# Two SwiGLU down projections in different forms, and the stores and sums of the gate stages on other engines

## The chip, the core and the metric

The kernel runs on one core of one Trainium2 chip. The metric is the device time of one execution in microseconds (us), median of several. The core has five engines that each work through a queue of their own in order: PE (TensorE, matmuls, with its weight loads PEld), DVE (VectorE), ACT (ScalarE), POOL (GpSimd) and SP (SyncE, which here issues nearly all DMAs). They meet through semaphores.

## The reference

A decoder trunk of two layers in float32, with 1024 tokens of 1024 features and an FF width of 2816. The first layer mixes tokens by sliding-window attention, the second by stick-breaking attention, and each is followed by a SwiGLU. Scales, shifts and gates of every sub-layer come from the conditioning `c` by `ada_w` (adaLN).

```python
def swiglu(h, w_gate, w_up, w_down):
    return (jax.nn.silu(h @ w_gate) * (h @ w_up)) @ w_down

def reference(x, c, ...):
    cond = jax.nn.silu(c)
    for i in range(DEPTH):                       # DEPTH = 2
        mod = (cond @ ada_w[i] + ada_b[i])[:, None, :]
        sh1, sc1, g1, sh2, sc2, g2 = jnp.split(mod, 6, axis=-1)
        h = rmsnorm(x, norm1_g[i]) * (1.0 + sc1) + sh1
        y = ...                                  # attention of layer i
        x = x + g1 * y
        h = rmsnorm(x, norm2_g[i]) * (1.0 + sc2) + sh2
        x = x + g2 * swiglu(h, w_gate[i], w_up[i], w_down[i])
    return x
```

## The kernel before, in words

Every matrix product is made of float32 operands split in two: ACT casts the high part (`sh` L629, `dah` and `dbh` L308), DVE subtracts it to get the low part (`sl` L630, `dal` and `dbl` L309), and three matmuls, high by high, high by low and low by high, stand for one (`mm3`, each matmul recorded at L108). The order of the matmuls is written out by hand and chained; the other engines' order comes from a scheduler that keeps to the order of the code where priorities don't differ. A pool of n buffers makes the n+1st user wait until the first is done.

A **gate stage** (`gates`, one for each layer) computes silu(h w_gate) * (h w_up) in 11 chunks of 256 FF columns. The product of a chunk is cut in 2 x 2 blocks, and seven block products stand in place of eight: seven for the gate and seven for the up weights, 12 matmuls each, 168 a chunk. On PE a chunk is three stretches by its PSUM banks: `psd` (X, 48 matmuls), `psz` (Y: T2, T3 and N4, 72) and `pst` (Z: T1 and B22, 48). POOL makes the sums of weight blocks that these products need, in the ring `rg` of seven buffers (`block_sums` L804 to L806, `t2_product` L812); DVE adds up the results (`u2` L814, `u3` L851, `p1` L854, L858, L861), and ACT and DVE make silu and product (L864, L865; `g11` L843, L844). The four results of a chunk, A11, A12, A22 and `g11`, lead to the seven left operands of the down projection: A11, A12 and A22 themselves, and the four sums S1 (POOL, L867), S2 (L871), S4 (L873) and S3 (L875). All seven are stored to DRAM by `store` (L829) on SP's queue.

At the start of each chunk `down_sums` (L902) loads two 128-row blocks of w_down (L907) into the pool `ad` of two 512 KB buffers, POOL makes four sums of their quarters (L910), and two stores on SP's queue bring them to DRAM (`wT`, L915 and L916). In layer 0 each chunk also issues five steps of the adaLN products that later stages need (`ada_step`, 56 in all): a load of 512 KB into the same pool `ad` (L262), an accumulation on DVE (L268, or L265 for the first of a group of eight), and after a group of eight some small matmuls against `ones`.

A **down projection** (`down` L918, the same code for both layers) is again seven block products, 924 matmuls: each loads a left operand from `hidS` and a right one from w_down or `wT` (L923, pool `raw` with five buffers), splits them, and multiplies over 22 FF blocks. The results are multiplied by the gate's row when they leave PSUM (L959) and added to the residual `xacc` (L964), the last of them just before `finish` stores a row block. After layer 0 `norm_b` (L1066) normalises each row block of the residual (L1074 on DVE) and transposes it on PE (L116) for the second layer's projections, whose weights are loaded and split ahead (L309, L312).

## Time and profile before

| | |
|---|---|
| median of the runs shown | 2538.48 us (3 runs: 2553.88, 2538.48, 2538.34) |
| the profiled execution's own time | 2545.3 us |
| its span in the profile | 2543.6 us |
| granted TensorE clock, mean | 0.96 of full speed |
| busy in the span: PE, DVE, ACT, POOL | 91%, 65%, 43%, 35% |
| gates of layer 0 | 479.67 to 960.88 us |
| first down projection, PE | 973.56 to 1186.20 us |
| gates of layer 1 | 1895.46 to 2319.60 us |
| second down projection, PE | 2326.66 us to the end |

The profile is of one execution. Its view by stretches gives busy time of each engine in each stretch, the number of instructions in brackets, the granted TensorE clock as a share of full speed, the DMA engines' share and the rate. The view of waits gives for each engine and line what it waited for: total, times and the longest. The timeline gives start, duration, engine, line, operation, output and inputs, with the idle time before it and what ended that in square brackets. A row of several instructions has an x and their count. PE's neighbouring matmuls overlap, so what one costs is read from a long row of them and not from its own duration. Names such as `f`, `p`, `rg` are those of tiles; `f` and `p` are results of a gate stage's products.

### The profile page before, as it was taken

How to read it: one execution, taken by the hardware profiler on the slowest of the kernel's cores; microseconds unless marked ns; L12 is line 12 of the kernel's file. 1: busy time of each engine (PE TensorE's matmuls, PEld its weight loads, DVE VectorE, ACT ScalarE, POOL GpSimd, SP SyncE). 2: the span in 40 equal slices, each digit the busy share in tenths (PEclk: the TensorE clock that was granted, in tenths of full speed). 3: DMA queues.
4: the chain of work that ended last, by engine and by line, in shares of the span. 5: the costliest groups of instructions: out<-in, count | busy, mean ns of one | idle time of the engine just before them, and what ended most of it. 6: DMA issues, size and time to landing. Idle time of an engine off the chain costs nothing. (4 is left out here: it accounts for less than half of the span.)

```text
span 2543.6 us, 31733 instructions
## 1 busy us (share of the span) xinstructions
PE 2326.9 (91%) x11140; PEld 1903.1 (75%) x11140; DVE 1642.7 (65%) x2315; ACT 1106.1 (43%) x2109; POOL 898.9 (35%) x847
## 2 busy tenths in 40 slices
PE   6798799799889897999999999998979989998999
PEld 6677677577777776887788888877758767887887
DVE  6678866855566665755676766687565645554864
ACT  4487733422222223433566666673343322333431
POOL 2443524234645530001244444441514574541000
PEclk9799899899999998999999999999979999999999
DMA  8113488345566547762222222236813564226753
GB/s 283 50 51 120 126 219 260 108 137 167 198 190 207 194 145 274 243 198 91 60 59 59 59 55 56 58 96 156 240 59 103 169 224 141 95 96 218 255 190 140
DMA packets 229855, 371.85 MB, mean 146 GB/s; under 512 B 15536, under 2 KB 135488, under 8 KB 229696
## 3 DMA queue, kind: packets, MB, share of 16 engines
q1 hardware_dynamic: 229072, 369.69, 46.2%
q8 instruction: 88, 1.44, 0.2%
q14 instruction: 71, 0.58, 0.1%
q10 hardware_dynamic: 624, 0.14, 0.0%
HBM read 264.39 MB, written 96.99 MB: 142 GB/s over the span
## 5 line engine op out<-in xcount | busy, mean ns | idle before, releaser
L629 ACT CAST sh<-rg 128x512 fp32r<-128x512 f32 x308 | 190.5, 622 | 644.8 <-PE psz L108 251.2
L630 DVE TENSOR_TENSOR sl<-rg,sh 128x512 fp32r<-128x512 f32 x308 | 289.5, 942 | 130.1 <-ACT sh L629 125.2
L108 PE MATMUL psd<-hth,whl 128*128 128x512 f32 x768 | 302.1, 412 | 0.1
L1182 POOL TENSOR_TENSOR bb<-bb,nb 128x895 f32<-128x895 f32 (+7 forms) x128 | 172.7, 1352 | 240.9 <-DVE nb L1180 152.2
L1180 DVE TENSOR_TENSOR_SCAN nb<-nb,ones 128x896 f32<-128x896 f32 (+7 forms) x128 | 194.1, 1519 | 45.2 <-ACT nb L1173 44.8
L108 PE MATMUL psz<-hT,sh 128*128 128x512 f32 x352 | 146.9, 420 | 50.5 <-DVE f L814 24.8
L804 POOL TENSOR_TENSOR rg<-rg,rg 128x512 f32<-128x512 f32 x44 | 60.7, 1380 | 340.5 <-DMA rg<-in_w_up_dram 262.3
L108 PEld LDWEIGHTS psd<-hth,whl 128*128 128x128 f32 x768 | 145.3, 189 | 21.5 <-issue 0.7
L308 ACT CAST dah<-raw 128x1024 fp32r<-128x1024 f32 x84 | 82.5, 982 | 165.5 <-PE psa L108 77.2
L108 PE MATMUL psd<-htl,whl 128*128 128x512 f32 x384 | 151.0, 395 | 0.0
L119 DVE TENSOR_TENSOR al<-pst,ah 128x512 fp32r<-128x512 f32 x160 | 108.4, 684 | 62.1 <-ACT ah L1203 59.0
L108 PE MATMUL psz<-lT,sh 128*128 128x512 f32 x352 | 146.1, 415 | 1.9 <-DVE lT L119 1.8
L108 PE MATMUL psz<-hT,sl 128*128 128x512 f32 x352 | 144.6, 411 | 1.2 <-DVE sl L630 1.2
L309 DVE TENSOR_TENSOR dal<-raw,dah 128x1024 fp32r<-128x1024 f32 x84 | 95.2, 1133 | 70.4 <-ACT dah L308 69.4
L108 PE MATMUL psd<-hB,sh 128*128 128x512 f32 x352 | 137.8, 391 | 2.3 <-ACT p L799 2.3
L108 PE MATMUL psd<-hB,sl 128*128 128x512 f32 x352 | 137.2, 390 | 1.2 <-DVE sl L630 1.2
L268 DVE SCALAR_TENSOR_TENSOR acc<-ada,condT,acc 128x1024 f32<-128x1024 f32 x77 | 106.5, 1384 | 49.1 <-DMA ada<-in_ada_w_dram 48.5
L108 PE MATMUL psd<-lB,sh 128*128 128x512 f32 x352 | 137.4, 390 | 0.0
L108 PEld LDWEIGHTS psz<-hT,sh 128*128 128x128 f32 x352 | 70.3, 201 | 74.9 <-issue 27.1
L309 DVE TENSOR_TENSOR dbl<-raw,dbh 128x1024 fp32r<-128x1024 f32 x84 | 95.0, 1131 | 44.4 <-ACT dbh L308 43.7
L1173 ACT ACTIVATE nb<-psz 128x448 f32<-128x448 f32 (+3 forms) x192 | 95.7, 498 | 60.4 <-PE psz L108 57.3
L1203 ACT CAST ah<-pst 128x512 fp32r<-128x512 f32 x160 | 94.0, 593 | 47.5 <-PE pst L116 45.5
(340 smaller groups left out, 6606.8 us busy)
## 6 DMA issues: line engine op xcount, KB each, us to landing
ada<-in_ada_w_dram SPq DMA_DIRECT2D x96, 512.0 KB, 4.5
dw<-in_w_down_dram SPq DMA_DIRECT2D x44, 512.0 KB, 4.2
rg<-in_w_gate_dram SPq DMA_DIRECT2D x44, 512.0 KB, 4.8
rg<-in_w_up_dram SPq DMA_DIRECT2D x44, 512.0 KB, 4.8
wT<-dw SPq DMA_DIRECT2D x44, 512.0 KB, 3.2
raw<-wT SPq DMA_DIRECT2D x40, 512.0 KB, 5.3
raw<-hidS SPq DMA_DIRECT2D x40, 512.0 KB, 4.4
hidS<-f SPq DMA_DIRECT2D x64, 256.0 KB, 2.1
```

The lines of the kernel that those rows point to most:

```text
L108: chained(nc.tensor.matmul(o, l, r, start=start, stop=stop, skip_group_check=more))
L119: return nc.vector.tensor_tensor(o, a, h.bitcast(F32), op=ALU.subtract)
L268: i = nc.vector.scalar_tensor_tensor(a, wt, condT[:, j : j + 1], a, op0=ALU.mult, op1=ALU.add)
L308: nc.scalar.copy(h, raw)
L309: (eng or nc.vector).tensor_tensor(l, raw, h.bitcast(F32), op=ALU.subtract)
L629: nc.scalar.copy(hv, src)
L630: nc.vector.tensor_tensor(lv, src, hv.bitcast(F32), op=ALU.subtract)
L804: nc.gpsimd.tensor_tensor(A[1, 0], A[1, 0], A[1, 1], op=ALU.add)
L1173: nc.scalar.activation(nb[:, s0 : s0 + e], pz[:, 0:e], AF.Sigmoid, scale=-1.0)
L1180: nc.vector.tensor_tensor_scan(rv, rv, ones[:, 0:1].to_broadcast([P, L]), initial=1.0, op0=ALU.mult, op1=ALU.mult)
L1182: nc.gpsimd.tensor_tensor(bb[:, 0 : L - 1], bb[:, 0 : L - 1], nb[:, 1:L], op=ALU.mult)
L1203: nc.scalar.copy(ah_, pt)
```

## The change

In layer 1 the stores of a gate stage (L829 in the kernel before, and `wT` L915 and L916) go from SP's to POOL's DMA queue, and the four sums S1 to S4 from POOL to DVE. In layer 0 `down_sums` and the four sums are no longer done, and the four results go to a DRAM list `hid` by SP's queue (L847 and L870 in the kernel after). The first down projection is `down_rounds`: six rounds over the 22 FF blocks (4, 4, 4, 4, 4 and 2), in each of which two loads of 512 KB a block (the block of `hid`, 128 rows of w_down), a multiplication of the w_down rows by the gate's row on DVE and two splits precede 16 groups of matmuls, 1056 in all; each group is added from PSUM to the residual on DVE, and `finish` follows a row block's last add. The second projection keeps the block products.

```diff
--- before.py
+++ after.py
@@ -826,9 +826,10 @@
 
         def chunk(c):
             def store(n, t):
-                nc.sync.dma_start(hidS[n, c // 2][:, c % 2], t)
-
-            down_sums(l, c)
+                nc.gpsimd.dma_start(hidS[n, c // 2][:, c % 2], t)
+
+            if l:
+                down_sums(l, c)
             if c == 0:
                 m = first["m"]
             else:
@@ -842,6 +843,8 @@
             g11 = tile_()
             nc.scalar.activation(g11, m[0]["X"], AF.Silu)
             tt(g11, m[1]["X"], g11, op=ALU.mult)
+            if l == 0:
+                nc.sync.dma_start(hid[2 * c][:, 0:512], g11)
             if c:
                 for x in m:
                     t2_product(p, x, H, tile_())
@@ -863,16 +866,21 @@
                 g = m[0][n]
                 nc.scalar.activation(g, g, AF.Silu)
                 tt(g, m[1][n], g, op=ALU.mult)
+                if l == 0:
+                    nc.sync.dma_start(hid[2 * c + i][:, j * 512 : j * 512 + 512], g)
+                    continue
                 if n == "p1":
-                    pt_(g11, g11, g, op=ALU.add)
+                    tt(g11, g11, g, op=ALU.add)
                     store("S1", g11)
                 store({"p1": "A22", "u3": "A12", "u2": "A11"}[n], g)
+            if l == 0:
+                return
             s2, s3, s4 = (m[1][n] for n in ("u2", "p1", "u3"))
-            pt_(s2, g11, m[0]["u2"], op=ALU.subtract)
+            tt(s2, g11, m[0]["u2"], op=ALU.subtract)
             store("S2", s2)
-            pt_(s4, m[0]["u3"], s2, op=ALU.subtract)
+            tt(s4, m[0]["u3"], s2, op=ALU.subtract)
             store("S4", s4)
-            pt_(s3, m[0]["p1"], s2, op=ALU.subtract)
+            tt(s3, m[0]["p1"], s2, op=ALU.subtract)
             store("S3", s3)
 
         row = None
@@ -912,8 +920,8 @@
         sb(b12, b22, b12)
         sb(b22, b22, b11)
         sb(b21, b21, b22)
-        nc.sync.dma_start(wT[0, c // 2][:, c % 2], r0)
-        nc.sync.dma_start(wT[1, c // 2][:, c % 2], r1)
+        nc.gpsimd.dma_start(wT[0, c // 2][:, c % 2], r0)
+        nc.gpsimd.dma_start(wT[1, c // 2][:, c % 2], r1)
 
     def down(l, rawp, nraw, dn, xacc, row, finish):
         tt = nc.vector.tensor_tensor
@@ -998,6 +1006,56 @@
             add(rows_of(X[i], 1), 4 + i, 1)
             finish(4 + i)
 
+
+    ROUNDS = (4, 4, 4, 4, 4, 2)
+
+    def down_rounds(l, rawp, nraw, dn, xacc, hid, row, finish):
+        f0 = 0
+        for r, n in enumerate(ROUNDS):
+            g = r % 2
+            T = []
+            for j in range(n):
+                f = f0 + j
+                t = []
+                for e, src in enumerate((hid[f], w_down[l][f * P : (f + 1) * P])):
+                    raw = rawp.tile([P, D], F32, tag="raw", name=nm("raw"), bufs=nraw)
+                    ld = nc.sync.dma_start(raw, src)
+                    if e:
+                        nc.vector.tensor_tensor(raw, raw, row, op=ALU.mult)
+                    h = dn.tile([P, D], F32R, tag=f"{'ab'[e]}h{g}{j}", name=nm("dh"), bufs=1)
+                    l_ = dn.tile([P, D], F32R, tag=f"{'ab'[e]}l{g}{j}", name=nm("dl"), bufs=1)
+                    t += split_into(h, l_, raw)
+                T.append(t)
+            f0 += n
+            if r == 0:
+                with tc.issue_after(ld.ins):
+                    load_acc(xacc)
+
+            def one(pb, b, h, j):
+                ah, al, bh, bl = T[j]
+                mm3(pb, ah[:, b * P : (b + 1) * P], al[:, b * P : (b + 1) * P],
+                    bh[:, h * 512 : (h + 1) * 512], bl[:, h * 512 : (h + 1) * 512], j == 0, j == n - 1)
+
+            def evict(pb, b, h):
+                xs = xacc[b][:, h * 512 : (h + 1) * 512]
+                nc.vector.tensor_tensor(xs, pb, xs, op=ALU.add)
+
+            if r == 0:
+                pbs = [bank(t) for t in BANKS]
+                for j in range(n):
+                    for i in range(8):
+                        one(pbs[i], i // 2, i % 2, j)
+                for i in range(8):
+                    evict(pbs[i], i // 2, i % 2)
+            for b in range(4 if r == 0 else 0, NB):
+                for h in range(2):
+                    pb = bank(BANKS[(2 * b + h) % 8])
+                    for j in range(n):
+                        one(pb, b, h, j)
+                    evict(pb, b, h)
+                if r == len(ROUNDS) - 1:
+                    finish(b)
+
     def mixer(l, W, p, od, x_src, gi, ada_per, rest, row):
         first = gates_first(l, p)
         H, cm_h2 = out_proj(p, W, od, x_src, l, gi, first, row)
@@ -1017,6 +1075,7 @@
         for b in range(NB):
             nc.sync.dma_start(xacc[b], xsp[b])
 
+    hid = [dr.tile([P, S], F32, name=f"hid{f}") for f in range(NF)]
     hidS = {(n, t): dr.tile([P, 2, 512], F32, name=f"hid{n}{t}") for n in LHS.values() for t in range(len(STEPS))}
     wT = {(i, t): dr.tile([P, 2, D], F32, name=f"wT{i}{t}") for i in range(2) for t in range(len(STEPS))}
     xsp = [dr.tile([P, D], F32, name=f"xsp{b}") for b in range(NB)]
@@ -1040,7 +1099,7 @@
     cm_dn, dn = pools.open("dn0", "right")
     NQ = 9
     xacc = [xq.tile([P, D], F32, tag="xq", name=nm("xa"), bufs=NQ) for _ in range(NB)]
-    down(0, rw, 5, dn, xacc, row2, lambda b: nc.sync.dma_start(xsp[b], xacc[b]))
+    down_rounds(0, rw, 5, dn, xacc, hid, row2, lambda b: nc.sync.dma_start(xsp[b], xacc[b]))
     pools.close(cm_rw)
     pools.close(cm_dn)
 
```

In the engines' order this moves the following. On SP in layer 0's gate stage, before, the stores of a chunk's results, the next load and stores of `down_sums` and the adaLN loads stood in this order:

```order
L829 DMA hidS_3790<-p_1269_6648 128x512
L907 DMA dw_6918<-in_w_down_dram 128x1024
L915 DMA wT_3796<-dw_6916 128x1024
L916 DMA wT_3802<-dw_6918 128x1024
L262 DMA ada_7210<-in_ada_w_dram 128x1024
L262 DMA ada_7213<-in_ada_w_dram 128x1024
L262 DMA ada_7216<-in_ada_w_dram 128x1024
L262 DMA ada_7219<-in_ada_w_dram 128x1024
```

On the same engine and in the same stage after the change, with the stores to `hid`:

```order
L870 DMA hid_3758<-f_5756 128x512
L262 DMA ada_5911<-in_ada_w_dram 128x1024
L262 DMA ada_5914<-in_ada_w_dram 128x1024
L870 DMA hid_3757<-f_5700 128x512
L262 DMA ada_6194<-in_ada_w_dram 128x1024
L262 DMA ada_6197<-in_ada_w_dram 128x1024
L262 DMA ada_6200<-in_ada_w_dram 128x1024
L262 DMA ada_6203<-in_ada_w_dram 128x1024
L847 DMA hid_3759<-f_6001 128x512
L262 DMA ada_6218<-in_ada_w_dram 128x1024
```

The two `wT` stores, which wait for POOL's sums, and the loads into the pool `ad` that are not the adaLN's are gone from before the adaLN loads.

On POOL in layer 1's gate stage, one chunk from its first `block_sums` to its last weight sums (in the chunk with sums of `down_sums` these stand in between, as before), before:

```order
L805 TENSOR_TENSOR rg_18703<-rg_18703 128x4x128
L805 TENSOR_TENSOR rg_18707<-rg_18707 128x4x128
L806 TENSOR_TENSOR rg_18705<-rg_18705,rg_18703 128x4x128
L871 TENSOR_TENSOR f_18516<-f_18493,f_18496 128x512
L873 TENSOR_TENSOR f_18570<-f_18552,f_18516 128x512
L875 TENSOR_TENSOR p_3577_18453<-p_3573_18434,f_18516 128x512
L806 TENSOR_TENSOR rg_18709<-rg_18709,rg_18707 128x4x128
L812 TENSOR_TENSOR rg_18703<-rg_18705,rg_18703 128x4x128
L812 TENSOR_TENSOR rg_18707<-rg_18709,rg_18707 128x4x128
```

The same chunk on POOL after the change, where L829 is a store on POOL's own queue:

```order
L805 TENSOR_TENSOR rg_18536<-rg_18536 128x4x128
L829 DMA hidA_3782<-f_18385 128x512
L805 TENSOR_TENSOR rg_18540<-rg_18540 128x4x128
L806 TENSOR_TENSOR rg_18538<-rg_18538,rg_18536 128x4x128
L829 DMA hidA_3776<-f_18329 128x512
L829 DMA hidS_3806<-f_18349 128x512
L829 DMA hidS_3788<-f_18403 128x512
L829 DMA hidS_3812<-p_3491_18286 128x512
L806 TENSOR_TENSOR rg_18542<-rg_18542,rg_18540 128x4x128
L812 TENSOR_TENSOR rg_18536<-rg_18538,rg_18536 128x4x128
L812 TENSOR_TENSOR rg_18540<-rg_18542,rg_18540 128x4x128
```

The three sums of the chunk before are gone from between the two L806, and four stores of that chunk stand there, with a fifth between the two L805 and two more ahead of these rows.

On DVE at the end of the first projection, before, where L959 and L964 bring a product to the residual, L312 and L309 split the next weights and L1074 scales a row block for the normalisation:

```order
L959 TENSOR_TENSOR tm_9766<-psd_9101,grow_5632 128x512
L964 TENSOR_TENSOR xa_8217<-xa_8217,tm_9766 128x512
L312 SCALAR_TENSOR_TENSOR whl_9787<-wr_9785,whl_9787 128x1024
L309 TENSOR_TENSOR whl_9792<-wr_9790,whl_9792 128x1024
L1074 TENSOR_SCALAR xa_8210<-xa_8210,ss_9796 128x1024
```

There after the change, where L1041 adds a group of a round and L1133 is the scaling:

```order
L1041 TENSOR_TENSOR xa_8047<-psz_9501,xa_8047 128x512
L1133 TENSOR_SCALAR xa_8045<-xa_8045,ss_9629 128x1024
L1041 TENSOR_TENSOR xa_8047<-pst_9509,xa_8047 128x512
L1041 TENSOR_TENSOR xa_8048<-psz_9518,xa_8048 128x512
L1133 TENSOR_SCALAR xa_8046<-xa_8046,ss_9635 128x1024
```

The scaling of a row block now stands between the adds of later row blocks.

## Rows read from the trace of the kernel before

**Rows 1.** By stretches: us, busy us (instructions) by engine, PEclk, DMA share, GB/s
```profile
479.67:960.88 481.21, 436.35 (x1866) 352.85 (x1866) 299.90 (x361) 124.95 (x208) 232.40 (x156) 0.95 0.54 175
960.88:973.56 12.68, 0.00 (x1) 0.01 (x1) 2.63 (x4) 2.09 (x2) 3.74 (x3) 0.69 0.66 236
973.56:1186.20 212.64, 212.60 (x924) 174.92 (x924) 130.18 (x149) 82.75 (x90) 0.00 (x0) 0.99 0.63 218
1186.20:1198.15 11.95, 6.73 (x33) 5.74 (x33) 11.02 (x15) 4.51 (x7) 5.72 (x9) 0.71 0.40 122
1895.46:2319.60 424.14, 407.64 (x1754) 333.82 (x1754) 229.63 (x294) 125.44 (x208) 212.82 (x151) 0.97 0.41 134
2319.60:2326.66 7.06, 0.00 (x0) 0.00 (x0) 2.35 (x3) 2.04 (x3) 3.74 (x3) 0.82 0.79 299
```

**Rows 2.** Chain of layer 1's gates, PE: start, duration, line, count
```profile
2254.31 16.32 PE psz L108 x72
```

**Rows 3.** Waits of PE, gates of layer 0: us, times, longest
```profile
PE psz L108 <- DVE f L814: 24.8, 6, 6.4
PE psz L108 <- DVE f L851: 17.9, 3, 6.3
```

**Rows 4.** Timeline of PE, end of an adaLN group in layer 0's gates
```profile
956.90 1.16 PE L108 MATMUL pst<-ones,acc 128*128 128x128 f32 x8
```

**Rows 5.** Waits of DVE, gates of layer 0
```profile
DVE acc L268 <- DMA ada<-in_ada_w_dram: 36.4, 23, 6.0
```

**Rows 6.** Tile ada, gates of layer 0: instructions, ns min/median/max
```profile
L268 DVE SCALAR_TENSOR_TENSOR acc<-ada,condT,acc x44: 1272/1285/2345, 481.9 to 947.0; 128x1024 f32<-128x1024 f32 x44
...
DMA to landing us min/median/max: 3.8/4.2/4.7
```

**Rows 7.** Waits of SP's DMA queue, gates of layer 0
```profile
SPq L916 <- POOL dw L910: 23.7, 8, 4.3
SPq L915 <- POOL dw L910: 21.9, 7, 4.7
...
SPq L262 <- DMA wT<-dw: 21.2, 11, 2.7
```

**Rows 8.** Timeline of SP's queue, first raw load of the first projection
```profile
966.81 0.38 SPq L923 DMA_DIRECT2D raw<-in_w_down_dram  x1
```

**Rows 9.** Tile dal: the low part of a split, ns min/median/max
```profile
L309 DVE TENSOR_TENSOR dal<-raw,dah x84: 683/1224/1227, 973.5 to 2509.5; 128x1024 fp32r<-128x1024 f32 x70, 128x512 fp32r<-128x512 f32 x14
```

**Rows 10.** Tile f: a 128x512 product on DVE, ns min/median/max
```profile
L865 DVE TENSOR_TENSOR f<-f,f x42: 676/685/1780, 493.8 to 2320.4; 128x512 f32<-128x512 f32 x42
```

**Rows 11.** Timeline of PE, first transposes after the first projection
```profile
1190.67 0.33 PE L116 MATMUL psa<-ident,xa 128*128 128x128 f32 x1 [4.45 <-DVE xa L1074]
```

**Rows 12.** Timeline of POOL, a chunk of layer 1 without down_sums
```profile
2170.32 1.29 POOL L871 TENSOR_TENSOR f<-f,f 128x512 f32<-128x512 f32 x1
2171.68 1.62 POOL L873 TENSOR_TENSOR f<-f,f 128x512 f32<-128x512 f32 x1
2173.27 1.79 POOL L875 TENSOR_TENSOR p<-p,f 128x512 f32<-128x512 f32 x1
2175.02 1.29 POOL L806 TENSOR_TENSOR rg<-rg,rg 128x512 f32<-128x512 f32 x1
```

**Rows 13.** Timeline of DVE and PE, same chunk: T3's low part, T3's first matmul
```profile
2178.86 0.95 DVE L630 TENSOR_TENSOR sl<-rg,sh 128x512 fp32r<-128x512 f32 x1
...
2183.43 0.39 PE L108 MATMUL psz<-hT,sh 128*128 128x512 f32 x1
```

**Rows 14.** Waits of PE, gates of layer 1
```profile
PE psz L108 <- ACT sh L629: 14.4, 3, 8.1
```

**Rows 15.** Timeline of POOL, a chunk of layer 1 with down_sums
```profile
2038.25 1.29 POOL L804 TENSOR_TENSOR rg<-rg,rg 128x512 f32<-128x512 f32 x1 [3.30 <-DMA rg<-in_w_gate_dram]
```

**Rows 16.** The store's line L829: issue ns, and landing
```profile
L829 SPq DMA_DIRECT2D hidS<-f x64: 319/320/339, 491.0 to 2323.9; - x64
...
DMA to landing us min/median/max: 2.0/2.3/5.7
```

## The prediction

> **What bounds the kernel now.** I read the busy table by stage first. In both block-product projections TensorE (PE) is hardly idle (212.60 us busy of 212.64 in the third line of [rows 1]), and in the gate stages it should be: one chunk of 256 FF columns is 168 matmuls, and where nothing waits 72 of them take 16.32 us [rows 2], 0.2267 us each, so 38.1 us a chunk. The reader is to see four places where the span is longer than that.
>
> Gates of layer 0: 1866 PE rows in 481.21 us, idle 481.21 − 436.35 = 44.9 us. Of these, 112 are the small matmuls that end the adaLN groups, eight in 1.16 us [rows 4], 16.2 us in all, and 1752 are products, 397.2 us. The floor is 414.4 with about 1 us of edges, the excess 66.8: 44.9 idle, 21.9 because the products ran at a lower granted clock (0.95 against 0.99 in the projection, same rows; 2.4 GHz is full). Layer 1: 1754 × 0.2267 = 397.6 of 424.14, excess 26.5 (16.5 idle, 10.0 clock). The starts of the projections, 12.68 and 7.06 us with PE empty. The stretch after the first projection, 11.95 us with 6.73 of PE.
>
> Then the waits say why. In layer 0 PE waits for sums on VectorE (DVE), 24.8 and 17.9 us [rows 3]. DVE itself stands, in its fixed order, at the adaLN accumulation L268 for its weight tile, 36.4 us in 23 pieces [rows 5]. Such a tile lands 4.2 us after its issue [rows 6], so the issue is late: SP's queue (SyncE issues nearly every DMA) stood at the two stores of the `down_sums` rows, which wait for POOL, 21.9 and 23.7 us, and at L262 for a tile of pool `ad` (two buffers) that such a store still held, 21.2 us [rows 7].
>
> **The change, part by part.**
>
> Layer 0, `down_sums` and the sums of gate results go. `ad` then belongs to the adaLN tiles alone, and SP meets no POOL wait before them; the order in the change section shows them behind stores that wait for DVE only. What is late next: in six chunks a group of eight accumulations (1.285 us each) stands before the sum that the T3 products wait for, with two buffers, so a tile lands every (4.2 + 1.285)/2 = 2.7 us and eight need some 22 us; the first tiles are prefetched, and most of the rest lies beside the X and T2 products. I work out 1.5 us of stall in each of six chunks, 9 us, with half as much again for the clock as in the rows above (21.9 on 44.9), and 3.5 for the odd waits of DVE's other work: 17 of 66.8 stay. −50. Bounds: −65 (all but edges) and 0 (nothing, were DVE's order itself the cause).
>
> Start of the first projection. The first raw load was issued at 966.81 [rows 8], behind the last stores, after POOL's sums. Now the loads of round 0 stand ahead of them, and PE waits for the last product on DVE plus one split and its lower part (1.22 us [rows 9]): 4 us instead of 12.7, −8.7. Bounds 0 and −12.
>
> Plain rounds: 22 blocks × 8 × 2 × 3 = 1056 matmuls instead of 924, 132 × 0.2267 = +29.9. Covers: a round of four blocks is 192 matmuls, 43.5 us; DVE has in it 16 adds into the residual (0.69 as the sums of that size [rows 10]), eight splits and four row products at 1.22, 25.7 us, and eight loads of 512 KB make 96 GB/s against 218 in the projection before [rows 1]. I cost these at nothing; if a round opened with 2 us of wait, five rounds would add 10, which is the upper bound.
>
> Its end. Before, PE stood 4.45 us [rows 11] for the first normalised row block, whose scaling came on DVE behind all adds and the splits of the next weights. Now each block is scaled right behind its adds, while PE still works on the next block, so the transposes follow the last matmul: 11.95 becomes 5, −7 (bounds −3 and −8).
>
> Layer 1's gates carry the risk. POOL loses the four sums and gets nine DMA issues in the two chunks that also have `down_sums` work late, and seven in the others. In a steady chunk the order shows three sums between the two L806 replaced by four stores. The sums took 2170.32 to 2175.02, 4.7 us [rows 12]; the second L806 and L812 lead to the split whose lower part ends at 2179.81, and T3 starts at 2183.43 [rows 13], 3.6 us later. With d as POOL's time per store, PE waits if 4d > 4.7 + 3.6, d > 2.1. In two chunks with `down_sums` (waits of 8.1 and less, 14.4 together [rows 14]) nothing is slack: 9d more, less four sums (5.1 to 6.3 us, I take 5.6), less 2.5 of the 3.3 us that L804 waits for its weights [rows 15], since their load no longer stands behind stores on SP: 9d − 8.1 each.
>
> No POOL store is in this trace, so d is bounded: below by the issue on SP, 0.32 us, above by a store's landing, 2.3 us median and 5.7 at most [rows 16]. I take 1.3, one POOL pass over the same 128x512 tile (the 1.29 us of [rows 12]), as POOL would have to write out a store in software much as it walks a tile. So 2 × (9 × 1.3 − 8.1) = +7. At 0.32 it is −10; at 3, 8 × (12 − 8.3) + 2 × 18.9 = +67. The stores also make POOL wait in order for DVE's products, with the block sums queued behind; but in the order they stand in the next chunk, when DVE is done. DVE gets 4 × 0.685 = 2.7 us a chunk [rows 10], hidden as it is busy 229.63 of 424.14 us.
>
> What speaks against this part is a rule of the Trainium skill, "SBUF — State Buffer", section "SBUF: two separate sides" with the one after it: a DMA issued on GpSimd's queue has its descriptors written by GpSimd, which is shut out while VectorE runs an operation in a two-port mode, so that a DMA of 620 ns alone takes about 3100 ns. By 620 ns layer 1 would be 2 × (5.6 − 8.1) = −5 instead of +7, by 3100 ns a little over the +67 of d = 3. The page also says that tensor_tensor has no two-port mode but contends with GpSimd when both inputs are in SBUF; the POOL sums at 1.29, 1.62 and 1.79 us in one chunk fit that, and no run here shows a store yet.
>
> Start of the second projection: 7.06 becomes 5, −2 (bounds 0 and −3).
>
> Sum: −50 − 8.7 + 29.9 − 7 + 7 − 2 = −30.8. The profiled execution took 2545.3 us (span 2543.6, both in the profile's table), so 2514.5 on its terms. It ran 6.8 above the median of 2538.5; the same 6.8 off gives 2507.7, about 2508.
>
> **Rivals.** A measurement of this kernel tells about 1% (25 us) from no change, so faster is below 2513, slower above 2564.
>
> B, POOL's store is nearly free (d = 0.32): layer 1 gains 10 in issue order and some 3 of clock instead of losing 7, 2488. For it: the SP row. Against: POOL has no 0.32 us operation on such a tile.
>
> C, layer 0 keeps its waits: 22 instead of 50 go, because DVE's own order with eight accumulations ahead of the u2 sum holds PE with or without a late load; 2508 + 28, about 2535. For it: two buffers need 22 us for eight tiles, more than the X products last. Against: what ended DVE's 36.4 us was the landing of a tile [rows 5], whose issue SP had held back [rows 7].
>
> D, slower: one mechanism, POOL held 3 us by each store, with the block sums and so the T2, T3 weights of layer 1 behind it in its queue. The price is +67 instead of +7, 2568, and half as much again of lower clock at most, 2600; I set 2580. It decides from 50d − 82.6 = 37.8, d = 2.4 us, on. For it: a store's median landing of 2.3 us, if POOL stayed with it so long. Against: an issuing engine need not wait for a landing, as SP's 0.32 us shows.
>
> **How the numbers follow.** Forecast 0.52 (own range 2485 to 2522: layer 0 between −65 and −40, d between 0.7 and 1.6; of it faster 0.38, same 0.14); B 0.17, all faster; C 0.18 (same 0.15, faster 0.03); D 0.13 (slower 0.11, same 0.02). Faster 0.58, same 0.31, slower 0.11. The range: B with layer 0 at its −65 ends at 2472; C with rounds opening at +10 and half of the tail's gain is near 2550, and 2556 leaves out most of D alone.
>
> **What would show it.** Right: the gates of layer 0 near 431 us, no POOL wait on SP there, L268 waiting under 15 us; 1056 matmuls in about 240 us with PE busy throughout; the start at 4 us; the transposes right behind the last round; POOL's store rows near 1.3 us and layer 1's gates near 431. Wrong: L268 still waiting 30 us with its issue on time (C); PE waiting for sh L629 in most chunks of layer 1 with stores of 2.4 us or more on POOL (D); idle PE at each round's first matmul.

## The result, and the profile after

The changed kernel took 2510.45 us (median of 4 runs, 2508.52 to 2516.31) against 2538.41 us of the kernel before: a ratio of 0.9874, 95% interval 0.9855 to 0.9893. The forecast was 2508, range 2472 to 2556. So the kernel is 1.3% faster, clear of noise. The profiled execution took 2510.11 us, its span is 2508.4. Behind the close total stand two errors in layer 1: its attention part grew by 10.6 us, for which the sum has no term, and its gates came near the forecast although the time of a store and the cost of the stores were both wrong.

The view by stretches of the changed kernel answers to [rows 1], in the same columns: up to layer 0's gates, gates, start of the first projection, its rounds, its end, the second layer's attention part, layer 1's gates, start of the second projection.

```profile
0.00:475.37 475.37, 393.70 (x2051) 321.02 (x2051) 357.37 (x791) 263.59 (x655) 159.38 (x266) 0.94 0.49 146
475.37:901.90 426.53, 418.11 (x1866) 340.82 (x1866) 281.65 (x361) 125.55 (x208) 116.45 (x79) 1.00 0.45 138
901.90:903.98 2.08, 0.19 (x1) 0.00 (x1) 1.75 (x3) 2.04 (x3) 0.00 (x0) 1.00 0.00 0
903.98:1146.14 242.16, 241.16 (x1057) 199.31 (x1058) 138.41 (x163) 48.61 (x52) 4.64 (x9) 0.99 0.34 118
1146.14:1149.75 3.61, 3.61 (x33) 3.37 (x32) 3.41 (x5) 1.45 (x2) 0.00 (x0) 1.00 0.54 188
1149.75:1857.65 707.90, 655.95 (x3593) 537.78 (x3592) 489.74 (x558) 423.96 (x858) 272.53 (x257) 0.97 0.31 85
1857.65:2284.90 427.25, 408.94 (x1754) 334.84 (x1754) 270.65 (x335) 125.41 (x208) 196.55 (x199) 0.98 0.41 135
2284.90:2291.25 6.35, 0.00 (x1) 0.01 (x1) 4.34 (x6) 2.05 (x3) 2.16 (x4) 0.74 0.45 165
```

Two stretches of the kernel before have no row in [rows 1]; here they are from its trace, the first and the attention part:

```profile
0.00:479.67 479.67, 396.21 (x2051) 322.44 (x2051) 354.29 (x789) 264.38 (x655) 171.44 (x274) 0.93 0.50 151
...
1198.15:1895.46 697.31, 655.50 (x3593) 538.64 (x3592) 481.35 (x553) 422.48 (x856) 269.02 (x251) 0.97 0.31 85
```

The difference stage by stage, with what was forecast:

| stage | before | after | measured | forecast |
|---|---|---|---|---|
| up to layer 0's gates | 479.7 | 475.4 | -4.3 | 0 |
| gates, layer 0 | 481.2 | 426.5 | -54.7 | -50 |
| start of first projection | 12.7 | 2.1 | -10.6 | -8.7 |
| first projection | 212.6 | 242.2 | +29.5 | +29.9 |
| its end | 11.95 | 3.6 | -8.3 | -7 |
| attention, layer 1 | 697.3 | 707.9 | +10.6 | 0 |
| gates, layer 1 | 424.1 | 427.3 | +3.1 | +7 |
| start of second projection | 7.1 | 6.4 | -0.7 | -2 |
| second projection | 216.9 | 217.2 | +0.2 | 0 |
| span | 2543.6 | 2508.4 | -35.2 | -30.8 |

The medians differ by 28.0, not 35.2: the profiled execution of the kernel before was a long one. A second profile of it, last of the experiments, shows where.

The waits of the changed kernel in layer 0's gates, of PE and of DVE, answer to [rows 3] and [rows 5]:

```profile
PE psz L108 <- DVE f L814: 8.1, 10, 2.2
```

```profile
DVE acc L268 <- DMA ada<-in_ada_w_dram: 17.2, 25, 1.5
```

PE's 24.8 us for L814 have become 8.1 in ten small pieces, in the six chunks with eight accumulations. Of its 17.9 us for L851 nothing is left within the stage; 5.6 of them ended as the stage began, and such a wait of 6.2 us (for L854, the same sum) stands there after the change too. The granted clock of the stage is full (1.00 against 0.95). The store's line, now on POOL, answers to [rows 16]; the third line and the fourth are what POOL waited for before a store in layer 1, the last is its landing:

```profile
L829 POOL DMA_DIRECT2D hidS<-f x32: 539/539/544, 1868.0 to 2288.2; - x32
L829 POOL DMA_DIRECT2D hidA<-f x21: 539/557/576, 1873.9 to 2286.7; - x21
...
  DVE p L868: 30.3, 9
  DVE f L868: 8.7, 2
...
DMA to landing us min/median/max: 2.3/2.6/7.3
```

So d, POOL's time per store, is 0.54 to 0.56 us at the median, not the 1.3 that the forecast took. The transposes follow the rounds' last matmul (1145.90) with no gap, where [rows 11] had 4.45 us:

```profile
1145.90 0.39 PE L108 MATMUL psa<-dh,dl 128*128 128x512 f32 x1
1146.14 0.60 PE L116 MATMUL psz<-ident,xa 128*128 128x128 f32 x4
```

And most of the 10.6 us of the attention part stand towards its end, where the output projection's rows are normalised: PE waits there 10.9 us in three pieces, and in the kernel before 2.2 in one. First POOL, then DVE, then PE of the changed kernel, in three fences:

```profile
1748.41 1.25 POOL L918 TENSOR_TENSOR dw<-dw 128x512 f32<-128x512 f32 x1 [7.43 <-DMA dw<-in_w_down_dram]
1749.75 0.22 POOL L671 TENSOR_SCALAR ss<-ss 128x1 f32<-128x1 f32 x1
1750.05 0.57 POOL L672 TENSOR_TENSOR ss<-ss,mhalf 128x1 f32<-128x1 f32 x1
1752.58 1.26 POOL L918 TENSOR_TENSOR dw<-dw,dw 128x512 f32<-128x512 f32 x1 [1.96 <-DMA dw<-in_w_down_dram]
1753.93 0.22 POOL L671 TENSOR_SCALAR ss<-ss 128x1 f32<-128x1 f32 x1
```

```profile
1750.65 0.75 DVE L673 TENSOR_SCALAR xt<-xt,ss 128x1024 f32<-128x1024 f32 x1 [2.70 <-POOL ss L672]
1754.84 1.74 DVE L673 TENSOR_SCALAR xt<-xt,ss 128x1024 f32<-128x1024 f32 x1 [3.43 <-POOL ss L672]
```

```profile
1751.46 0.47 PE L116 MATMUL psd<-ident,xt 128*128 128x128 f32 x1 [6.25 <-DVE xt L673]
1756.63 0.47 PE L116 MATMUL psd<-ident,xt 128*128 128x128 f32 x1 [3.20 <-DVE xt L673]
```

POOL also does the two tiny norm operations L671 and L672 for each row block. A sum of the second chunk's w_down rows (L918), which waits for its load, now stands ahead of them in POOL's queue, and DVE and PE wait in turn. In the kernel before that second chunk's sums came behind all four pairs.

### The profile page after: what moved, and what is told of

Same layout as the page of the kernel before. It is cut to its first block, busy times and chain, and to the rows that moved or that the text cites. A ratio compares the mean times of both kernels' runs of the same rounds, so it can differ in the third digit from the quotient of the medians.

```text
span 2508.4 us, 31639 instructions
## 1 busy us (share of the span) xinstructions
PE 2333.4 (93%) x11272; PEld 1911.5 (76%) x11272; DVE 1678.6 (67%) x2369; ACT 1070.2 (43%) x2069; POOL 751.7 (30%) x814
## 4 chain that ended last, share of the span: by engine, by line
PE 65%; DVE 12%; DMA 8%; issue 6%; POOL 6%; ACT 3%; SPq 0%; ACTq 0%; POOLq 0%; DVEq 0%
PE psz L108 21%; PE psd L108 20%; PE pst L108 15%; PE psa L108 6%; DMA ada<-in_ada_w_dram 3%; PE pst L116 3%; DVE acc L268 2%; DVE nb L1239 2%; DMA dw<-in_w_down_dram 2%; POOL dw L918 1%; DMA wT<-dw 1%; DVE sl L630 1%; DVE al L119 1%; DVE Wl L309 1%; DVE lT L119 1%
## 5 line engine op out<-in xcount | busy, mean ns | idle before, releaser
L630 DVE TENSOR_TENSOR sl<-rg,sh 128x512 fp32r<-128x512 f32 x308 | 265.9, 864 | 67.8 <-ACT sh L629 67.7
L108 PE MATMUL psz<-hT,sh 128*128 128x512 f32 x352 | 141.7, 406 | 31.3 <-DVE f L814 13.4
L108 PE MATMUL psz<-lT,sh 128*128 128x512 f32 x352 | 141.0, 400 | 2.4 <-DVE lT L119 2.4
L268 DVE SCALAR_TENSOR_TENSOR acc<-ada,condT,acc 128x1024 f32<-128x1024 f32 x77 | 110.5, 1435 | 34.6 <-DMA ada<-in_ada_w_dram 33.6
L108 PE MATMUL psz<-QK,QK 128*128 128x384 f32 (+4 forms) x384 | 104.0, 353 | 1.7 <-ACT bb L1233 1.7
L308 ACT CAST dh<-raw 128x1024 fp32r<-128x1024 f32 x44 | 44.2, 1049 | 139.8 <-PE psa L108 86.6
L108 PE MATMUL psa<-al,V 128*128 128x256 f32 x320 | 87.5, 295 | 13.5 <-DVE al L119 12.5
```

The costliest lines, as they stand in the source:

```text
L108: chained(nc.tensor.matmul(o, l, r, start=start, stop=stop, skip_group_check=more))
L268: i = nc.vector.scalar_tensor_tensor(a, wt, condT[:, j : j + 1], a, op0=ALU.mult, op1=ALU.add)
L308: nc.scalar.copy(h, raw)
L630: nc.vector.tensor_tensor(lv, src, hv.bitcast(F32), op=ALU.subtract)
```

## The experiments

Stages are compared in the profiles; times are medians, with the kernel before on the same chip beside them.

**Only the first layer's part.** The changed kernel with layer 1 as before.

```diff
-                nc.gpsimd.dma_start(hidS[n, c // 2][:, c % 2], t)
+                nc.sync.dma_start(hidS[n, c // 2][:, c % 2], t)
...
-            tt(s2, g11, m[0]["u2"], op=ALU.subtract)
+            pt_(s2, g11, m[0]["u2"], op=ALU.subtract)
...
-        nc.gpsimd.dma_start(wT[0, c // 2][:, c % 2], r0)
+        nc.sync.dma_start(wT[0, c // 2][:, c % 2], r0)
...
```

> The changed kernel with layer 1's gate stage as it was before: stores on SP's queue, sums on POOL. My theory, from the two traces: in the changed kernel POOL's order in layer 1 puts sums of a second chunk of w_down rows, which wait for their load, between the small norm operations L671/L672, and that is the 10.6 us by which the second layer's attention part grew (697.3 to 707.9 us, from 1149.75 to 1857.65); with the stores back on SP that part is 697 again, the gates 424 instead of 427, the time about 14 below the changed kernel, 2497. Rival: the 10.6 us come from the first layer's part (the normalisation moved forward and the splits of the next weights behind it): the part stays at 708, the time at 2507 to 2511.

It took 2499.32 us (before: 2541.47; ratio 0.9834, 0.9818 to 0.9849). Attention part and gates of layer 1:

```profile
1149.12:1845.92 696.80, 653.61 (x3594) 535.38 (x3592) 488.48 (x558) 424.39 (x858) 272.59 (x251) 0.98 0.32 87
...
1845.92:2269.29 423.37, 406.10 (x1754) 332.90 (x1754) 222.34 (x294) 125.44 (x208) 212.71 (x151) 0.98 0.41 134
```

Both are back, 11.1 and 3.9 us, as the theory had it. The half of the change that is in layer 1 makes the kernel slower.

**Only the wT stores back on SP.** The last two lines of that edit alone.

> The changed kernel with only the two wT stores a chunk back on SP's queue; the seven others stay on POOL's, the sums on DVE. If the placement of the w_down sums before the norm is what costs (it comes with wT on POOL), the attention part goes back to 697 us and most of the 14 us is won: 2499. If the seven stores on POOL and the sums on DVE cost by themselves, 9d more per chunk with d = 0.55 us, the gates of layer 1 stay at 427 or longer and the time is 2500 to 2505. Rival as above: nothing changes, 2510.

2502.97 us (0.9847, 0.9833 to 0.9862). The attention part:

```profile
1149.58:1849.38 699.80, 654.58 (x3593) 535.96 (x3592) 487.65 (x558) 424.33 (x858) 271.77 (x251) 0.98 0.32 86
```

So of the 11.1 us there, 8.1 came with the wT stores on POOL (707.9 to 699.8) and 3.0 with the rest (by two runs below, the seven other stores: 696.8 us with the sums alone on DVE, 699.5 with these stores alone on POOL); the order of L918 and L671 is again that of the kernel before. The gates stay at 427.4: what costs there is in the seven stores or the sums.

**Only the engines, in both layers.** The kernel before with all gate-stage stores on POOL's queue and the four sums on DVE, block products kept.

> The kernel before with only the engines changed, in both layers: all stores of the gate stages on POOL's queue, the four sums on DVE, block products and w_down sums in both layers. In layer 0 SP then meets no store that waits for POOL ahead of the adaLN loads, but the two buffers of pool ad are still shared. If SP's queue was the main cause of the adaLN waits, the gates of layer 0 fall from 481 to about 445 us; if the shared buffers were, they stay at 465 or more. Layer 1 should look as in the changed kernel (708 and 427 us). Time by the first 2517, by the second 2540.

2544.48 us (before 2541.47; ratio 1.0009, 0.9997 to 1.0021): no gain. Layer 0's gates, and what SP waited for in them:

```profile
483.70:962.30 478.60, 437.85 (x1866) 352.10 (x1866) 340.94 (x402) 125.36 (x209) 208.62 (x206) 0.95 0.54 178
```

```profile
SPq L262 <- DMA wT<-dw: 138.3, 18, 13.9
```

SP's waits at stores for POOL are gone, the gates are not shorter: SP now stands 138 us at the adaLN loads themselves, for buffers that hold w_down rows until their `wT` stores, now in POOL's queue, have landed. DVE waits 44.1 us for adaLN tiles, more than before (36.4). The start of the first projection is 1.8 us. In layer 1 the attention part is 704.1 us and the gates 425.7, near the 708 and 427 that were expected.

**Layer 0 without the w_down sums.**

```diff
-            down_sums(l, c)
+            if l:
+                down_sums(l, c)
...
+        if l == 0:
+            return w_down[l].rearrange("(c i p) n -> i p c n", i=2, p=P)[i][:, c0 : c0 + n, dh * 512 : dh * 512 + 512]
```

> The kernel before without the w_down sums of layer 0: the loads, POOL's sums and the stores to wT are left out there, and the first projection reads rows of w_down in place of the sums (so many bytes as before); block products and the seven stores on SP stay. If the w_down sums in adaLN's buffers and on SP are the whole cause of layer 0's excess, its gates are about 430 us as in the changed kernel, and the time is 50 below before, 2488. If the four sums on POOL and the seven stores have a part of it, the gates are 445 to 460 us and the time 2503 to 2518. The start of the first projection stays at about 12 us in both.

2512.15 us (0.9881, 0.9867 to 0.9896). The gates:

```profile
479.68:930.30 450.62, 424.80 (x1866) 345.81 (x1866) 299.05 (x359) 125.71 (x208) 184.31 (x120) 0.98 0.45 142
```

30.6 of 54.7 us. The other 24 belong to the four sums or the stores, to which the next two runs speak.

**The same, with layer 0's seven stores on POOL's queue.**

> As the run without the w_down sums in layer 0 (loads, sums and wT stores left out there, rows of w_down read in place of the sums), and in layer 0 the seven stores of each chunk on POOL's queue; the four sums stay on POOL. That run kept 450.6 us of gates, 24 more than the changed kernel, with PE waiting 25.0 us in ten pieces for the u2 sum, all in chunks with eight adaLN accumulations. If SP's queue, which stood at stores that wait for POOL's sums, made the adaLN tiles late there, the gates of layer 0 fall to about 430 us, DVE's wait for adaLN tiles from 28.1 us to below 18, and the start of the projection to about 2 us. If the sums on POOL or the transfers themselves are the cause, the gates stay at 445 to 451.

One run, 2497.57 us. The gates are 444.5 us, 6 of the 24 less. DVE's wait for adaLN tiles fell to 6.7 us, as by the first theory, yet the gates stayed where the second had them, and PE still waited 14.9 us for DVE's u2 sum.

**The same as two above, without layer 0's four sums.**

```diff
-                    pt_(g11, g11, g, op=ALU.add)
+                    (pt_ if l else skip)(g11, g11, g, op=ALU.add)
...
-            pt_(s2, g11, m[0]["u2"], op=ALU.subtract)
+            (pt_ if l else skip)(s2, g11, m[0]["u2"], op=ALU.subtract)
...
```

> The run without the w_down sums in layer 0, and there the four sums of gate results left out too (the tiles that they would have filled are stored unsummed, the seven stores stay on SP). Layer 0's gates kept 450.6 us without the w_down sums and 444.5 with the stores on POOL's queue as well; the changed kernel has 426.5. If the sums are the rest of it, by POOL's use of what DVE needs (DVE's low parts L630 took 0.68 us where POOL was idle and 1.0 to 1.5 beside a POOL operation) and by SP's waits for POOL, the gates fall to 427 to 431 and DVE's busy time from 299 to about 282 us. If the seven stores' own transfers are it, they stay at 445 or more.

One run, 2478.66 us. The gates:

```profile
474.69:900.56 425.87, 418.06 (x1866) 340.87 (x1866) 276.33 (x359) 125.67 (x208) 115.24 (x79) 1.00 0.48 153
```

All 24.7 us are gone, with stores still on SP: they came with the four sums on POOL. DVE's busy time fell by 22.7 us for the same 359 instructions, so these sums had lengthened DVE's operations. SP's stand at stores that wait for the sums (72.2 us before this edit) went with them, so how much of the 24.7 either brought is not told apart.

**Layer 1: sums on DVE, stores on SP; and sums on POOL, stores on POOL.** Two edits of the first experiment's kernel, each one half of the change.

> The changed kernel's first layer; in layer 1 the four sums on DVE, all stores on SP's queue. Layer 1's gates were 423.4 us with sums on POOL and stores on SP, and 427.4 with sums on DVE and seven stores a chunk on POOL. If the sums on DVE are what costs the 4 us (PE then waits for DVE's u2 sum L814, which it did for 6.6 us in the latter and not in the former), the gates are about 427 here; if the stores on POOL are, about 420, as POOL loses four sums of 1.3 us a chunk and gets nothing.

> The changed kernel's first layer; in layer 1 the seven stores a chunk on POOL's queue (0.54 us each), the four sums on POOL as before, wT stores on SP. If the stores on POOL are what costs 4 us, the gates of layer 1 are 427 us or more: POOL gets 7 x 0.54 = 3.8 us a chunk on top of its sums; in the two or three chunks in which POOL is late that is 4 us each, 431 to 435. If the sums on DVE are the cost, they are 423.

One run each, 2483.55 and 2509.96 us. Layer 1's gates, sums moved first, stores moved second, each kernel in a fence of its own:

```profile
1844.66:2257.35 412.69, 406.31 (x1754) 333.13 (x1754) 258.19 (x335) 125.50 (x208) 157.07 (x110) 0.98 0.41 138
```

```profile
1847.07:2283.02 435.95, 408.60 (x1754) 334.29 (x1754) 273.48 (x294) 125.48 (x208) 242.71 (x224) 0.97 0.39 132
```

| gates of layer 1 | sums on POOL | sums on DVE |
|---|---|---|
| seven stores on SP | 423.4 | 412.7 |
| seven stores on POOL | 436.0 | 427.4 |

By both expectations it is the stores that cost, 12.6 us (14.7 with the sums on DVE), and the sums on DVE gain 10.7 (8.5 with stores on POOL), three times what was expected of them. The changed kernel, 427.3 us, is the fourth field with the `wT` stores on POOL besides. In the kernel with stores on POOL, POOL between the two L806 of a chunk, and in a second fence PE behind it:

```profile
1999.68 1.28 POOL L806 TENSOR_TENSOR rg<-rg,rg 128x512 f32<-128x512 f32 x1
2000.90 0.56 POOL L829 DMA_DIRECT2D hidA<-f  x1
2001.48 1.27 POOL L879 TENSOR_TENSOR f<-f,f 128x512 f32<-128x512 f32 x1
2003.05 0.56 POOL L829 DMA_DIRECT2D hidS<-f  x1 [0.30 <-POOL f L879]
...
2007.16 1.27 POOL L806 TENSOR_TENSOR rg<-rg,rg 128x512 f32<-128x512 f32 x1
```

```profile
2012.17 0.77 PE L108 MATMUL psz<-hT,sh 128*128 128x512 f32 x1 [10.73 <-DVE f L814]
```

The second L806, on which weights of this chunk's T2 and T3 products rest, starts 7.5 us behind the first, with 2.2 us of stores among the sums. The weights' split and DVE's u2 sum follow it, and PE stands 10.7 us, where the first experiment's kernel had 8.0 in the same chunk.

**Pacing.** The first experiment's kernel with layer 1's w_down loads queued behind the next chunk's weight load.

```diff
...
                 m = [load_chunk(p, w, c) for w in (w_gate[l], w_up[l])]
+                if l:
+                    with tc.issue_after(p["ld"].ins):
+                        down_sums(l, c - 1)
+                        if c == NC - 1:
+                            down_sums(l, c)
...
```

> The changed kernel's first layer; layer 1 with stores on SP and sums on POOL as in the kernel before, and with the w_down loads of each chunk queued behind the weight load of the next chunk, so that the sums come once a chunk and not bunched in chunks 0 to 6. My theory: the two waits of PE of about 8 us in layer 1's gates come from bunched sums on POOL ahead of the weight sums. Spread out, POOL has four sums more (5.2 us) in each of its 38 us chunks and slack for them, so both waits and the clock behind them go: gates 403 to 408 instead of 423.4, the attention part 697 or a few less, time 2480 to 2486. Rival: POOL has no slack in any chunk, and the 16 us come back as small waits in all of them: 420 to 425, time 2496 to 2502.

2490.75 us (before 2540.65; 0.9803, 0.9785 to 0.9820), gates 417.2 us. The result lies between the theory and its rival: the two long waits are gone, but PE waits for `sh` in eight small pieces (9.9 us, the longest 3.9).

**Pacing and sums on DVE.**

> The changed kernel's first layer; in layer 1 stores on SP, the four sums on DVE, and the w_down loads of a chunk queued behind the next chunk's weight load. Layer 1's gates were 423.4 us with neither, 412.7 with the sums on DVE, 417.2 with the pacing alone. If both act on the same shortage, POOL being late with the weight sums, and neither uses it up, the gates are 402 to 407 and the time 2474 to 2480; if the pacing adds nothing once POOL has room, they are 411 to 414 and the time 2483 to 2487.

2479.67 us (before 2539.6; 0.9765, 0.9744 to 0.9786), gates of layer 1:

```profile
1845.73:2252.37 406.64, 403.81 (x1754) 329.53 (x1754) 286.70 (x336) 124.67 (x208) 187.31 (x123) 1.00 0.45 156
```

Both act; within the stage PE hardly waits. Of the kernels that do the whole computation this is the fastest, ahead of both kernels of the change.

**Block products in both layers, w_down rows in buffers of their own.**

```diff
-            r = ad.tile([P, D], F32, tag="ad", name=nm("dw"), bufs=2)
+            r = ad.tile([P, D], F32, tag="ad", name=nm("dw"), bufs=2) if l else dwp[0].tile([P, D], F32, tag="dw", name=nm("dw"), bufs=2)
...
```

> Block products in both layers as in the kernel before, with three changes: in layer 0 the w_down rows have two buffers of their own (taken from the gate results' pool, eight buffers in place of twelve there), in both layers their loads are queued behind the next chunk's weight load, and the four sums are on DVE; all stores on SP. If the adaLN tiles' two buffers, shared with the w_down rows, were the larger part of layer 0's excess, its gates are 428 to 440 us with all the w_down work in them, and the time 12 to 25 below the changed kernel with sums on DVE and stores on SP (2483.5), as the block products save 29 us of matmuls, with some 8 us given back at the end of the first projection: 2458 to 2472. If POOL's sums or the transfers were, the gates stay at 455 us or more and the time above 2480.

2484.19 us (0.9784, 0.9762 to 0.9806). Layer 0's gates:

```profile
475.97:919.70 443.73, 422.17 (x1866) 341.82 (x1866) 347.14 (x400) 124.91 (x208) 191.88 (x123) 0.99 0.58 196
```

With all the w_down work in it the stage is 35 us shorter than with the engines alone changed, and DVE's wait for adaLN tiles is 6.4 us in place of 44.1. That fits separate buffers, but the paced loads and the stores back on SP came along, and the shares are not told apart. The total missed its 2458 to 2472: the gates are 19 us longer than the 424.7 of the run before this, and the start of the projection (11.3) and its end (12.3) came back. Plain rounds are 4.5 us ahead of block products here, but the two intervals overlap, so which is better is not settled.

**The kernel before again.**

> The kernel before once more, for a second profile of it. Its first profiled execution took 2545.3 us, 6.8 above the median that went with it, and the stages of the two profiles differ by 35.2 us where the medians differ by 28.0. If the difference lies in layer 0's gates, whose waits hang on DMA queues, this profile has them at 474 to 479 us instead of 481.2 and the other stages within 1 us; if it is spread over the stages, no stage differs by more than 3 us.

2536.25 us. Layer 0's gates and the attention part:

```profile
479.93:954.90 474.97, 433.13 (x1866) 351.08 (x1866) 300.46 (x361) 124.83 (x208) 230.95 (x156) 0.95 0.53 177
...
1192.16:1886.05 693.89, 652.81 (x3594) 537.57 (x3592) 484.86 (x552) 422.23 (x856) 270.80 (x251) 0.98 0.31 86
```

Layer 0's gates differ by 6 us between the two executions and the attention part by 3.4, the other stages by less than 0.6: the expectation named the first of the two alone. Against this profile the gates gained 48.4 us and the attention part lost 14.

## Why the prediction was right or wrong

Right as forecast: the rounds (132 matmuls, +29.5 for +29.9, PE busy 241.16 of 242.16, so nothing of their adds and loads showed), the start of the first projection, its end, and what the layer 0 gates would keep (12.1 us over the floor of 414.4, where 17 were expected, with the waits in the chunks that were named). One sign was missed narrowly: L268 still waits 17.2 us for its tiles, where under 15 was named. That the total came within 3 us is in part luck: the +10.6 of the attention part, in no term of the sum, was offset by -4.3 in front of layer 0's gates, also in no term, and by the two gate stages, 4.7 and 3.9 us better than forecast.

Layer 0's -54.7 (-48.4 against the second profile) agrees with -50, but its reason holds in part only. The step that failed is that the adaLN loads are issued late because SP's queue stands at the two stores of `down_sums`, which wait for POOL. With those stores moved to POOL's queue the gates stayed at 478.6 and SP stood at the buffers of `ad` instead; that run moved the wait, and put stores on POOL besides, so it does not weigh the two causes. With buffers of their own for the w_down rows, and pacing, DVE waited 6.4 us for tiles although SP still stood 35.2 us at the `wT` stores for POOL, which speaks for the buffers. Nor do late tiles set the length of the stage: 6.7 us of waiting for them go with gates of 444.5 us, 18.1 us (without the four sums) with 425.9.

Only 30.6 us hang on the w_down sums at all (24.4 against the second profile). The other 24.7 came with the four sums of gate results, which the prediction names in half a sentence and to which it gives no cost of their own. That they cost it is shown; how is argued. They lengthen DVE's own operations, and DVE is what PE waits for in the six chunks with eight accumulations; they also hold SP at the stores of their results. Taking these stores off SP gave 6 us, but put them on POOL, where DVE became busier still (329.7 us against 299.1), so the two are not separated.

Layer 1's gates came out at +3.1 for +7, by two errors against each other. The step was 9d - 8.1 in two chunks, with d = 1.3. With the measured d of 0.54 it gives 2 x (4.9 - 8.1) = -6. Its sums half was about right (11.2 us for four sums in two chunks, measured 8.5 to 10.7). Its store half was mis-sized: 7 stores cost 12.6 to 14.7 us for 2 x 7 x 0.54 = 7.6 of POOL's time. The wT stores cost nothing there (427.3 with them, 427.4 without). POOL's waits for DVE at its stores, which the prediction put at nothing, are not the cause. The 30.3 us for L868 above have a counterpart in layer 1's gates of the kernel before, where POOL waited for the same product at the sum S1; and in the run with the stores moved alone, POOL waits 2.9 us for DVE at them.

```profile
POOL f L867 <- DVE p L865: 28.2, 9, 17.2
```

What it left out is that DVE is lengthened too: 222.3 us busy in the first experiment, 273.5 with the stores on POOL, for 294 instructions each. Of these 51 us, 47 lie in 16 low parts L630 that take 2.9 to 6.5 us each in place of 0.68. Of the 12.6 us that the stores cost, 10.1 are idle time of PE (27.4 against 17.3): 4.4 in the two long waits behind POOL's queue (10.7 and 9.5 against 8.0 and 7.8), 2.9 directly behind two such low parts, here first DVE's rows and then PE's, and the rest in smaller waits. The other 2.5 us fit the lower clock (0.97 against 0.98).

```profile
1946.74 6.48 DVE L630 TENSOR_TENSOR sl<-rg,sh 128x512 fp32r<-128x512 f32 x1 [1.33 <-ACT sh L629]
1953.14 4.88 DVE L630 TENSOR_TENSOR sl<-rg,sh 128x512 fp32r<-128x512 f32 x1
```

```profile
1953.27 0.50 PE L108 MATMUL psd<-hB,sl 128*128 128x512 f32 x1 [1.15 <-DVE sl L630]
1958.08 0.50 PE L108 MATMUL psz<-hT,sl 128*128 128x512 f32 x1 [1.77 <-DVE sl L630]
```

The attention part of layer 1 was not in the sum at all. The prediction looked for what stands behind a store on POOL in the gate stage and not where the scheduler, with stores elsewhere, would put the w_down sums of the first two chunks: 8.1 us for their place before L671, 3.0 for the rest. Against the second profile some 3 us more come with layer 0's part: with layer 1's stores on SP the attention part took 692.3 to 693.9 us in five of six profiles of kernels with block products (697.3 in the first) and 696.8 to 698.2 in the four with plain rounds. Why was not followed. The 4.3 us in front of layer 0's gates stay open: without the w_down sums the stretch was 479.7 us as before, without the four sums as well 474.7, but also 476.8 with these sums kept and only the seven stores off SP.

Of the rivals, C did not come (layer 0 kept 12 us). B had the better d and the wrong consequence. D's mechanism, POOL held in order with the block sums behind its stores, is a part of what layer 1 shows, at a sixth of its d. D's threshold comes to d = 2.5 and not 2.4, since the +7 that is already in 2508 has to come out first; nothing hangs on it.

## What to carry to other kernels

When a change moves many things, price it by stage and by half: here layer 0's part was worth about 42 us (2541.47 to 2499.32), layer 1's sums on DVE another 11 in the gates, and its stores on POOL's queue took 26 back (14.7 in the gates, 11.1 in the attention part). Stores that are moved to a computing engine's queue stand in the order of that engine's work, change how its work meets that of other engines, and let a scheduler reorder the rest; read the new order at the stages before and behind as well. Before replacing an algorithm because its side work hurts, try to move the side work: paced loads and sums on DVE were worth 17 us in layer 1 alone.

## What the runs showed of the hardware

A store of 128x512 floats issued by POOL occupies POOL for 0.54 to 0.56 us at the median, one of 128x1024 (wT) for 0.57, where SP's issue of the former took 0.32; the former lands in 2.6 us at the median against 2.3. POOL does not wait for the landing.

DVE's operations on two SBUF tiles grow beside POOL's sums. In the run without w_down sums and with layer 0's stores on POOL, DVE and then POOL over the same stretch:

```profile
675.99 3.40 DVE L268 SCALAR_TENSOR_TENSOR acc<-ada,condT,acc 128x1024 f32<-128x1024 f32 x1 [0.56 <-DMA ada<-in_ada_w_dram]
679.31 1.90 DVE L630 TENSOR_TENSOR sl<-rg,sh 128x512 fp32r<-128x512 f32 x1
...
688.73 0.68 DVE L630 TENSOR_TENSOR sl<-rg,sh 128x512 fp32r<-128x512 f32 x1
```

```profile
675.75 1.30 POOL L874 TENSOR_TENSOR f<-f,f 128x512 f32<-128x512 f32 x1
677.00 1.30 POOL L876 TENSOR_TENSOR p<-p,f 128x512 f32<-128x512 f32 x1
...
678.80 0.54 POOL L829 DMA_DIRECT2D hidS<-p  x1
679.35 1.29 POOL L806 TENSOR_TENSOR rg<-rg,rg 128x512 f32<-128x512 f32 x1
681.28 2.27 POOL L812 TENSOR_TENSOR rg<-rg,rg 128x512 f32<-128x512 f32 x1 [0.64 <-DVE sl L630]
```

The low part L630 takes 0.68 us where POOL is idle (688.73) and 1.90 beside POOL's L806, 0.6 us beyond its end; the accumulation, 1.285 us as a rule [rows 6], takes 3.40 and ends 1.1 us behind the two sums L874 and L876. So DVE hardly moves while such sums run, and when POOL goes from one to the next it can stand through both. A store's issue alone does not do this: beside one and no sum, 34 L630 of three kernels with stores on POOL took 0.68 to 0.69 us. Yet the long ones come only where POOL issues stores: in every gate stage without any, in all 14 profiles, no DVE operation on two SBUF tiles takes more than 2.5 us, and with seven stores a chunk on POOL the longest takes 6.48. Why DVE gets in between POOL's sums without the stores and not with them was not followed. Summed over the 145 L630 of layer 1's gates it is 130.1 us with sums on POOL and stores on SP, and 180.6 with the stores on POOL as well.

The Trainium skill, "SBUF — State Buffer", section "Who interferes with whom", says that tensor_tensor with both inputs in SBUF contends with GpSimd's reads, and the rows of L630 agree. Its other rule, weighed in the prediction, that DVE starves the descriptors of GpSimd's DMAs from 620 to some 3100 ns, is not put to the test here: it is about two-port modes of DVE, and all of DVE's operations in layer 1's gates are tensor_tensor, which by the same section has no such mode. POOL's 128x512 stores took 539 to 653 ns there, beside a DVE busy 63% of the stage (270.65 of 427.25 us).
